# The sixth product's weight sums in five seven-product halves: all added by GpSimd, instead of two by VectorE and three by adding DMAs

## The chip, the cores and the metric

The kernel runs on one core of a Trainium2 chip. The metric is the device time of one execution in microseconds (us); lower is better. The core has a matrix engine (TensorE; PE in the profile, with PEld for its weight loads), VectorE (DVE), ScalarE (ACT), GpSimd (POOL) and SyncE (SP). DMAs that SyncE issues go through one queue, DMAs that GpSimd issues through another.

## The reference

One layer of an encoder block over 256 tokens and a width of 2048, in float32. The input `x` is normalised and multiplied by `w_in`. The eight parts of the result feed a recurrent branch (convolution, gates, two scans), an attention branch, and two merge gates. Both branches are projected, gated, added and multiplied by `w_out`.

```
xn = rms_norm(x, norm_pre_w)
u, g_lru, q, k, v, g_attn, m_lru, m_attn = split(xn @ w_in)
h   = rg_lru(conv(u), forward) + rg_lru(conv(u), backward)
y_a = h * silu(g_lru)
y_b = windowed_gqa(rope(q), rope(k), v, sink) * silu(g_attn)
merged = sigmoid(m_lru) * (y_a @ w_proj_a) + sigmoid(m_attn) * (y_b @ w_proj_b)
out = x + rms_norm(merged @ w_out, norm_post_w)
```

## The kernel before

All weights stream through once, in steps whose order is written out by hand in the strings `START`, `MERGE` and `OUT`. A step is a "block" or a "quad" of 128x2048 weights, or a "part" of the same size in a group of seven products. Each step is worked in two halves of 128x1024. For each half, ScalarE casts the raw weights to a high part `wh` (line 219), VectorE subtracts to get the low part `wl` (line 221), and PE multiplies with both. In the main loop, the cast of half `hs + 4` and the subtraction of half `hs + 3` are issued while half `hs` is multiplied, and loads are issued 3 to 5 steps ahead. Further work (convolutions, scans, attention heads, evacuations) is hung on time steps of this loop. Engines run their instructions in the order in which they are recorded.

Five halves of matrix products, named L, M, N, A (the two merge gates' columns of `w_in`) and O (half of the columns of `w_out`), are done with seven products in place of eight. Each has four blocks of weights, and some of the seven products need sums of these blocks. The sums grow in place in two cells, "x" and "y", each in two parts (0 and 1) of two tiles of 128x1024 (a and b). So `Lx0a` is tile a of part 0 of cell x of group L. SyncE loads a fresh block into a cell; the next blocks are added to it by DMAs that GpSimd issues with `accum_op=ALU.add` (line 192). Each DMA moves one tile, 512 KB.

- Cell x serves products m5, m6 and m4 in turn (in L, M, N and A its first block serves m1 too).
- Cell y is loaded fresh with the block of m3; later m7 adds to it.
- For m6, cell x needs the very block that lies fresh in cell y for m3.

In groups A and O, the table `ADDED` makes VectorE add cell y's tile to cell x's (line 224), right after it has split that tile for m3. In L, M and N the block is read from HBM a second time, by four adding DMAs per group. The split of a tile for m6 by ScalarE and VectorE waits for its sum.

The line that chooses, in `fetch`, and the add, in `split`, are in the functions printed here.

Of the kernel before, what the change touches and what calls it, by code (L numbers as in the profile page):

```python
# [18 lines left out]
ALU = mybir.AluOpType  # L19
# [50 lines left out]
LRU = (-4, 0, 2, 2, 2, 2, 2, 4)  # L70
QUADS = {"u": ("w_in", U0), "v": ("w_in", V0), "p": ("w_proj_a", 0),
         "b": ("w_proj_b", 0), "o": ("w_out", 0)}
ADDED = {'A': {'m3': 'm6'}, 'O': {'m3': 'm6'}}
PAIRS = {"g": GL0, "h": GA0, "w": U0, "k": K0, "q": Q0}
SEVENS = {"L": ("w_in", ML0 + 1024), "M": ("w_in", ML0), "N": ("w_in", MA0), "A": ("w_in", MA0 + 1536), "O": ("w_out", 0)}

# [10 lines left out]
def load_plan():  # L87

    plan = []
    for o in START + MERGE + OUT:  # L90
        a, i = o.split(".")
        if a[0] in SEVENS:
            plan.append(("part", a[0], a[1:], int(i)))
        elif a[0] in PAIRS:
            n = int(a[1:]) * (4 if a[0] == "q" else 1) + int(i)
            plan.append(("blk", "w_in", PAIRS[a[0]] + n * P, 0))
        else:
            w, c = QUADS[a[0]]
            plan.append(("quad", w, c + int(a[1:]) * 512, int(i)))
    return plan  # L100
# [15 lines left out]
def body(ctx, tc, x, x0, xT, wall, wlru, pvec, npost, ident_d, mask_d, rope_d, out):  # L116
    nc = tc.nc
# [8 lines left out]
    def unit(name, dt=F32, shape=(P, 4, S)):  # L126
        return units.tile(list(shape), dt, tag="u", name=name)
# [27 lines left out]
    plan = load_plan()  # L155
# [31 lines left out]
    def load(cell, p, add=False):  # L187

        w = wall[row[content(p)]]
        for h in range(2):  # L190
            if add:
                nc.gpsimd.dma_start(flat(cell[h]), w[:, h * 1024:(h + 1) * 1024], accum_op=ALU.add)
            else:
                nc.sync.dma_start(flat(cell[h]), w[:, h * 1024:(h + 1) * 1024])
# [3 lines left out]
    def chained(i):  # L198
        return plan[i][0] == "part" and groups[plan[i][1]].where(plan[i][2]) != "z"

    def fetch(i, lead):
        if i >= len(plan):
            return
        if plan[i][0] == "part":
            groups[plan[i][1]].fetch(plan[i], lead)
        if lead == 3 and i not in raws and not chained(i):
            nc.sync.dma_start(flat(raw_tile(i)), wall[row[content(plan[i])]])

    def split(q, c=0, w=1024, cast=nc.scalar.copy, only=None):
        i, h = q // 2, q % 2  # L210
        if i >= len(plan):
            return
        if c == 0 and only != "l":
            parts[q] = [unit(f"w{s}{i}_{h}", F32R, (P, 1024)) for s in "hl"]
        wh, wl = parts[q]
        cell = groups[plan[i][1]].cell(*plan[i][2:]) if chained(i) else raws[i]
        hs, ls, raw = wh[:, c:c + w], wl[:, c:c + w], flat(cell[h])[:, c:c + w]
        if only != "l":
            cast(hs, raw)  # L219
        if only != "h":  # L220
            nc.vector.tensor_tensor(ls, raw, hs.bitcast(F32), ALU.subtract)  # L221
            if plan[i][0] == "part" and plan[i][2] in ADDED.get(plan[i][1], ()):
                x = flat(groups[plan[i][1]].cells["x", plan[i][3]][h])
                nc.vector.tensor_tensor(x, x, raw, ALU.add)

    def mm3(ps, wh, wl, xh, xl, start, stop, more=False):

# [113 lines left out]
    def x_sum(name, s, q):  # L341
        t = unit(name, F32R, (P, 4, 2, P))
        nc.sync.dma_start(t.rearrange("p a b c -> p a (b c)").bitcast(F32), away[q][:, SUMS.index(s)])
        return t

    class Seven:
# [22 lines left out]
        def fetch(self, p, lead):  # L369
            m, q = p[2:]  # L370
            fresh = ("m1", "m3") if self.sums is None else ()
            if self.sums is None:
                if lead == 4 and m in fresh:
                    self.start(self.where(m), q)
                if lead == 4 and SEVEN[m][0][0] == "s":
                    self.kept[m, q] = x_sum(f"{self.name}{m}{q}", SEVEN[m][0], q)
            if lead == 5 and m in ("m5", "m6", "m7", "m4")[self.sums is not None:] and m not in ADDED.get(self.name, {}).values():
                load(self.cell(m, q), p, True)

        def start(self, where, q):  # L380
# [109 lines left out]
    for j in range(4):  # L490
        if j == 0:
            scale_x(0, 0, lambda: split(0, 0, 512, nc.vector.tensor_copy, "h"))
            split(0, 0, 512, only="l")
        else:
            scale_x(0, j)
            split(j // 2, j % 2 * 512, 512)
# [370 lines left out]
    def head(hd, qh, ql, b, both, end):  # L867
# [73 lines left out]
        if j % 2 == 1:  # L941
            for d, fn in enumerate((send, None, fetch, None, None, p_parts, None, None, values, gate_out), 6):
                if fn:
                    at(b + d, fn)
            if g > 1:
                at(max(b + 16, end + hd // 2 - 4), lambda: yb_parts(hd // 2))
# [196 lines left out]
    for i, (kind, half) in enumerate(steps):  # L1143
        for h in range(2):
            new = h == 0 or kind != "part"
            tick += new
            now[0], hs = tick, 2 * i + h
            if h == 0:
                for lead in (3, 4, 5):
                    fetch(i + lead, lead)  # L1150
            if new and tick in first:
                first.pop(tick)()
            if hs < FIRST:
                split(hs + 4)
            if new:
                for fn in due.pop(tick, ()):
                    fn()
            if hs >= FIRST:
                split(hs + 4, only="h")
                if hs > FIRST:  # L1160
                    split(hs + 3, only="l")
            if new and tick in last:
                last.pop(tick)()
            half(h, *parts.pop(hs))
# [72 lines left out]
```

## Time and profile before

| | |
|---|---|
| median of 3 runs | 877.22 us (876.87 to 877.27) |
| the profiled execution | 876.5 us, span 874.7 us |
| PE / VectorE / ScalarE / GpSimd busy | 864.9 / 728.6 / 643.1 / 66.1 us |
| adding DMAs on GpSimd's queue | 72, 37.75 MB |
| GpSimd's adds of two tiles | 1 (128x512, in the tail) |
| HBM read | 228.24 MB |

The span is the profiled part of an execution; the time of the whole execution lies 1.8 us above it. A row of a group names line, engine, operation, and `out<-in` by the kernel's tile names. A row of the timeline begins with start and length in us, and a number in square brackets is the idle time before it with what ended it. A row of a tile view gives shortest, median and longest duration in ns and the first and last start in us. In a row of stretches the busy times are those of PE, PEld, VectorE, ScalarE and GpSimd, each with its count of instructions, then PE's clock, the DMA share and GB/s.

### The profile page before, as it was taken

Reading aid. Unit: us, or ns where it says so; the run is one execution under the profiler, and the core shown is the slowest. Engines: PE = TensorE matmul, PEld = TensorE weight load, DVE = VectorE, ACT = ScalarE, POOL = GpSimd, SP = SyncE. Lnnn points to the kernel's source line nnn. Section 1 sums busy time; section 2 is a strip of 40 time slices with the busy share of each in tenths; the row PEclk is TensorE's granted clock in tenths of the full one; section 3 lists DMA queues with packets and bytes.
Section 4 is the critical chain, followed back from the end, with each engine's and each line's share of the span. In section 5 each row is a group of like instructions: output and inputs, shape, how many; then the busy total and the mean of one; then the engine's idle time right before and its main releaser. Section 6 shows DMA issues by size and latency. Waiting matters only on the chain.

```text
span 874.7 us, 12312 instructions
## 1 busy us (share of the span) xinstructions
PE 864.9 (99%) x4474; PEld 741.7 (85%) x4474; DVE 728.6 (83%) x975; ACT 643.1 (74%) x929; POOL 66.1 (8%) x97
## 2 busy tenths in 40 slices
PE   9999999999999999999999999999999999999996
PEld 8888888888888888888888888888888888888885
DVE  6898999898887989779677788988678778778885
ACT  7689687877888696887777699976567456555654
POOL 0000001012000011100001200000000101000200
PEclk9999999999999999999999999999999999999999
DMA  9757699999959999996999987999989988968772
GB/s 332 276 194 236 202 362 244 361 332 291 336 186 278 319 298 316 302 314 230 277 345 305 303 297 218 333 326 309 303 323 364 297 269 261 315 248 353 188 198 96
DMA packets 63390, 247.92 MB, mean 283 GB/s; under 512 B 6241, under 2 KB 19297, under 8 KB 47841
## 3 DMA queue, kind: packets, MB, share of 16 engines
q1 hardware_dynamic: 52384, 208.59, 64.6%
q0 software_dynamic: 10368, 37.75, 22.2%
q10 hardware_dynamic: 576, 0.79, 0.3%
q8 instruction: 35, 0.57, 0.2%
q14 instruction: 27, 0.21, 0.1%
HBM read 228.24 MB, written 18.87 MB: 283 GB/s over the span
## 4 chain that ended last, share of the span: by engine, by line
PE 94%; issue 3%; DMA 2%; ACT 0%; POOLq 0%; DVE 0%; SPq 0%; ACTq 0%
PE ga L255 7%; PE q L255 7%; PE gl L255 7%; PE u L255 5%; PE Am L410 4%; PE Mm L410 4%; PE Lm L410 4%; PE Nm L410 4%; PE ga L253 3%; PE q L253 3%; PE gl L253 3%; PE Om L410 3%; PE u L253 3%; PE pa__6025 L275 2%; PE pa__5514 L275 2%
## 5 line engine op out<-in xcount | busy, mean ns | idle before, releaser
L221 DVE TENSOR_TENSOR wl<-raw,wh 128x1024 fp32r<-128x1024 f32 (+1 forms) x252 | 299.1, 1203 | 56.5 <-ACT wh L219 43.9
L219 ACT CAST wh<-raw 128x1024 fp32r<-128x1024 f32 (+1 forms) x251 | 253.7, 1036 | 67.5 <-DMA raw<-wall_dram 39.6
L255 PE MATMUL ga<-xs,wh 128*128 128x512 f32 x256 | 63.5, 391 | 0.0
L255 PE MATMUL gl<-xs,wh 128*128 128x512 f32 x256 | 63.4, 391 | 0.0
L255 PE MATMUL q<-xs,wh 128*128 128x512 f32 x256 | 63.2, 391 | 0.0
L255 PEld LDWEIGHTS q<-xs,wh 128*128 128x128 f32 x256 | 47.0, 188 | 9.1
L255 PEld LDWEIGHTS gl<-xs,wh 128*128 128x128 f32 x256 | 47.0, 188 | 9.0
L255 PEld LDWEIGHTS ga<-xs,wh 128*128 128x128 f32 x256 | 46.7, 188 | 8.8
L255 PE MATMUL u<-xs,wh 128*128 128x512 f32 x192 | 47.5, 391 | 0.0
L255 PEld LDWEIGHTS u<-xs,wh 128*128 128x128 f32 x192 | 35.2, 188 | 6.7
L253 PEld LDWEIGHTS q<-xs,wl 128*128 128x128 f32 x256 | 33.2, 191 | 1.2
L253 PE MATMUL q<-xs,wl 128*128 128x256 f32 x256 | 34.0, 283 | 0.0
L253 PEld LDWEIGHTS ga<-xs,wl 128*128 128x128 f32 x256 | 33.0, 191 | 1.2
L253 PEld LDWEIGHTS gl<-xs,wl 128*128 128x128 f32 x256 | 32.8, 191 | 1.2
L253 PE MATMUL ga<-xs,wl 128*128 128x256 f32 x256 | 33.5, 283 | 0.0
L253 PE MATMUL gl<-xs,wl 128*128 128x256 f32 x256 | 33.2, 283 | 0.0
L253 PEld LDWEIGHTS u<-xs,wl 128*128 128x128 f32 x192 | 24.6, 191 | 0.9
L253 PE MATMUL u<-xs,wl 128*128 128x256 f32 x192 | 24.9, 283 | 0.0
L662 DVE SCALAR_TENSOR_TENSOR uu<-upad,pv,uu 128x256 f32<-128x256 f32 x48 | 23.2, 483 | 1.7
L746 ACT ACTIVATE sig<-sg 128x512 f32<-128x512 f32 x16 | 10.2, 635 | 14.1 <-DVE sg L589 14.1
L148 ACT CAST ms<-mt 128x512 fp32r<-128x512 f32 x8 | 4.7, 588 | 20.0 <-PE mt L989 20.0
L230 PE MATMUL gate<-ul,lwl 128*128 128x256 f32 x64 | 18.1, 283 | 0.0
(513 smaller groups left out, 2097.5 us busy)
## 6 DMA issues: line engine op xcount, KB each, us to landing
raw<-wall_dram SPq DMA_DIRECT2D x121, 1024.0 KB, 7.9
lraw<-wlru_dram SPq DMA_DIRECT2D x8, 512.0 KB, 6.3
away<-xx SPq DMA_DIRECT2D x8, 512.0 KB, 8.7
Lm<-away SPq DMA_DIRECT2D x8, 512.0 KB, 11.2
Mm<-away SPq DMA_DIRECT2D x8, 512.0 KB, 13.4
Nm<-away SPq DMA_DIRECT2D x8, 512.0 KB, 14.2
turn<-pt SPq DMA_DIRECT2D x32, 128.0 KB, 4.4
pl<-turn SPq DMA_DIRECT2D x8, 512.0 KB, 7.2
```

The costliest lines, as they stand in the source:

```text
L148: nc.scalar.copy(h, src)
L219: cast(hs, raw)
L221: nc.vector.tensor_tensor(ls, raw, hs.bitcast(F32), ALU.subtract)
L230: nc.tensor.matmul(ps, wl, xh, start=False, stop=stop, skip_group_check=more)
L253: nc.tensor.matmul(ps[:, 1], wl[:, sl], a[:, 0], start=False, stop=False)
L255: nc.tensor.matmul(ps, wh[:, sl], a, start=k == 0, stop=k == KT - 1)
L275: nc.tensor.matmul(got[t], a[:, i], (wl if low else wh)[:, sl], start=k + low + i == 0, stop=low == 1 and k == KT - 1)
L410: nc.tensor.matmul(self.ps[b], a[i], (wl if low else wh)[:, sl], start=fresh and j + low + i == 0, stop=last and j + low == 2, skip_group_ ...
L662: nc.vector.scalar_tensor_tensor(u, up[:, j, tap:tap + S], cw[:, tap:tap + 1], u, ALU.mult, ALU.add)
L746: nc.scalar.activation(sg, dst, AF.Sigmoid)
```

## The change

`ADDED` no longer names groups: for every group, the tile of m3 is added to cell x, and no adding DMA is issued for m6. The add moves from VectorE to GpSimd, at the same place in the program.

```
-ADDED = {'A': {'m3': 'm6'}, 'O': {'m3': 'm6'}}
+ADDED = {"m3": "m6"}
...
             nc.vector.tensor_tensor(ls, raw, hs.bitcast(F32), ALU.subtract)
-            if plan[i][0] == "part" and plan[i][2] in ADDED.get(plan[i][1], ()):
+            if plan[i][0] == "part" and plan[i][2] in ADDED:
                 x = flat(groups[plan[i][1]].cells["x", plan[i][3]][h])
-                nc.vector.tensor_tensor(x, x, raw, ALU.add)
+                nc.gpsimd.tensor_tensor(x, x, raw, ALU.add)
...
-            if lead == 5 and m in ("m5", "m6", "m7", "m4")[self.sums is not None:] and m not in ADDED.get(self.name, {}).values():
+            if lead == 5 and m in ("m5", "m6", "m7", "m4")[self.sums is not None:] and m not in ADDED.values():
                 load(self.cell(m, q), p, True)
```

GpSimd's queue in group L, first before, then after. `upad` is the padded buffer of the convolution, the first `Lx` rows before are the adding DMAs for m6, and the `Ly` rows those for m7.

```order
L582 MEMSET upad_1782 128x2x2
L583 MEMSET upad_1782 128x2
L192 DMA Lx0a<-wall_dram 128x1024
L192 DMA Lx0b<-wall_dram 128x1024
L192 DMA Lx1a<-wall_dram 128x1024
L192 DMA Lx1b<-wall_dram 128x1024
L192 DMA Ly0a<-wall_dram 128x1024
```

```order
L582 MEMSET upad_1782 128x2x2
L583 MEMSET upad_1782 128x2
L224 ISA
L224 TENSOR_TENSOR Lx0a<-Lx0a,Ly0a 128x1024
L224 TENSOR_TENSOR Lx0b<-Lx0b,Ly0b 128x1024
L224 TENSOR_TENSOR Lx1a<-Lx1a,Ly1a 128x1024
L224 TENSOR_TENSOR Lx1b<-Lx1b,Ly1b 128x1024
L192 DMA Ly0a<-wall_dram 128x1024
```

Four adds stand where four DMAs stood; the same exchange is made in M and N. The ISA row, which loads GpSimd's code for such adds, stood before the add in the tail and now stands before the first add of L. In A and O four adds are new in GpSimd's queue, ahead of the `Ay` and `Oy` DMAs.

VectorE's queue in group A, around the split of `Ay0a` and `Ay0b`, before:

```order
L221 TENSOR_TENSOR wl_0_6669<-Ay0a,wh_0_6668 128x1024
L224 TENSOR_TENSOR Ax0a<-Ax0a,Ay0a 128x1024
L934 TENSOR_TENSOR sga_6162<-o_6660,sga_6162 128x512
L149 TENSOR_TENSOR yb_6658<-sga_6162,yb_6658 128x2x256
L221 TENSOR_TENSOR wl_1_6679<-Ay0b,wh_1_6678 128x1024
L224 TENSOR_TENSOR Ax0b<-Ax0b,Ay0b 128x1024
```

The two rows of line 224 are gone from it after the change; the rest stands in the same order. O loses its four in the same way.

## The prediction

> **What bounds the kernel now.** I read the page first, then the waits of the matrix engine, then stretches of the span.
>
> ```profile
> PE 864.9 (99%) x4474; PEld 741.7 (85%) x4474; DVE 728.6 (83%) x975; ACT 643.1 (74%) x929; POOL 66.1 (8%) x97
> ...
> PE spin L452 <- POOL eps L454: 1.0, 1, 1.0
> PE u_ps L557 <- ACT xs L486: 0.5, 1, 0.5
> PE u_ps L557 <- ACT wh L219: 0.3, 1, 0.3
> ...
> 35.00:866.00 831.00, 831.00 (x4287) 712.40 (x4286) 699.93 (x933) 614.57 (x885) 63.71 (x84) 1.00 0.88 283
> ```
>
> The first row is the page's busy time, the next three are all of PE's waits, and the last is one stretch of 831 us (columns: length; PE, PEld, DVE, ACT, POOL busy; PE clock; DMA share). PE is busy for all 831.00 us of it at clock 1.00. Its only waits are 1.8 us at the very start. So PE's work is the time, and nothing that is made lighter on another engine or queue can shorten those 831 us. A change can lose time, by making a weight tile arrive later than PE's need of it. What has to be known is how far VectorE (DVE), which makes the low part `wl` of each weight tile, runs ahead of PE, and what the change does to that lead.
>
> **The removed transfers.** Twelve adding DMAs go: two parts of two tiles in each of L, M and N.
>
> ```profile
> q0 software_dynamic: 10368, 37.75, 22.2%
> ...
> ACT wh L219 <- DMA raw<-wall_dram: 39.6, 18, 6.5
> ```
>
> The kernel has 72 of these DMAs (37.75 MB at 512 KB each). Twelve are a sixth: 22.2% / 6 = 3.7% of the 16 DMA engines' span. Some of ScalarE's 39.6 us of waiting for raw tiles may go with them. PE waits for none of it (rows above), so I cost this at nothing; the cover is PE's own work, and if it were gone the gain could not pass ScalarE's 39.6 us.
>
> **The adds taken off VectorE.** In A and O, eight adds of one tile leave it:
>
> ```profile
> L224 DVE TENSOR_TENSOR Ax0a<-Ax0a,Ay0a x1: 1226/1226/1226, 676.6 to 676.6; 128x1024 f32<-128x1024 f32 x1
> ...
> L1108 POOLq MODIFY_POOL_CONFIG  x2: 366/366/366, 840.2 to 840.2; - x2
> L1108 POOLq EVENT_SEMAPHORE  x1: 17/17/17, 847.3 to 847.3; - x1
> L1108 POOL TENSOR_TENSOR yw<-yw,xr x1: 1265/1265/1265, 869.1 to 869.1; 128x512 f32<-128x512 f32 x1
> ...
> L454 POOL MEMSET eps<- 128x1 f32 x1 | 0.1, 99 | 0.0
> ```
>
> 8 x 1.22 = 9.8 us of VectorE, none of it on PE's path: worth nothing by itself. It comes too late to help the stretch of A below, whose first add on VectorE starts at 676.6.
>
> **The adds on GpSimd.** Twenty come, four in each of five groups. The trace has one GpSimd add of two operands, half as wide: 1.265 us. With about 0.10 us of fixed start (the smallest memset, 99 ns), a tile of 1024 columns takes 0.10 + 2 x 1.165 = 2.43 us, 49 us in all on an engine that is 8% busy. Ahead of the first one stands the loading of GpSimd's code, which before sat at 840.2 and let the next wait end at 847.3, 7.1 us later.
>
> ```profile
> L192 POOL DMA_DIRECT2D Lx1b<-wall_dram x3: 874/881/888, 149.2 to 224.3; - x3
> L194 SPq DMA_DIRECT2D Ly0a<-wall_dram x1: 327/327/327, 170.0 to 170.0; - x1
> DMA to landing us min/median/max: 9.0/9.6/10.3
> ...
> 208.38 1.07 ACT L219 CAST wh<-Lx0a 128x1024 fp32r<-128x1024 f32 x1
> ```
>
> GpSimd's last DMA of the fifth product's first use is at 149.2, and the first add needs `Ly0a`, which lands at 170.0 + 9.0 = 179.0. The code load has 30 us of cover; it costs nothing. The sums are needed from 208.4 on, when ScalarE casts `Lx0a`. Two adds after 179 and two after the next pair of tiles has landed are done before that, so they do not come late by themselves. Queued behind the four adds on GpSimd are the seventh product's adding DMAs and, in L, two memsets of the convolution's next buffer.
>
> ```profile
> L219 ACT CAST wh<-Ny0a x2: 1047/1052/1058, 468.5 to 503.2; 128x1024 fp32r<-128x1024 f32 x2
> L192 POOL DMA_DIRECT2D Ny0a<-wall_dram x1: 862/862/862, 472.7 to 472.7; - x1
> DMA to landing us min/median/max: 9.2/9.3/9.4
> ...
> 198.76 0.44 POOL L582 MEMSET upad<- 128x4 f32 x1
> ...
> 221.36 0.69 DVE L593 TENSOR_TENSOR upad<-u,upad 128x512 f32<-128x512 f32 x1
> ```
>
> N is the tightest: `Ny0a` went out at 472.7 and is cast at 503.2. Behind four adds it goes out some 8 us later, near 481, and lands 9.4 us on, 13 us ahead of the cast. The memset at 198.8 has until 221. Both cost nothing while these covers stand; gone, each would cost what it is late.
>
> **What the adds do to VectorE.** This is the term that decides. Both engines would read two operands from SBUF at the same time. The trace of before shows no such overlap, so it gives bounds only. Let h be the time for which one GpSimd add keeps VectorE from working. If they pass each other freely, h is 0. If GpSimd holds what VectorE needs for a whole add, h is 2.43. Between them lies the case where they meet only for one stream of the tile's columns, for which the nearest row is VectorE's own add of such a tile, 1.22. VectorE is nearly full where the adds fall, and the lead over PE is short. Each stretch below runs from the landing of the first fresh tile to the weight tile with the shortest lead (in A, `Ay0a` lands at 659.4 + 7.3 = 666.7):
>
> ```profile
> L194 SPq DMA_DIRECT2D Ay0a<-wall_dram x1: 332/332/332, 659.4 to 659.4; - x1
> DMA to landing us min/median/max: 7.3/9.2/11.1
> ...
> 179.00:195.00 16.00, 16.00 (x92) 14.10 (x91) 15.55 (x21) 11.44 (x15) 1.74 (x2) 1.00 1.03 346
> 318.00:341.00 23.00, 23.00 (x125) 20.00 (x124) 21.28 (x26) 19.02 (x23) 3.49 (x4) 1.00 1.05 316
> 458.00:471.00 13.00, 13.00 (x72) 11.30 (x71) 12.27 (x15) 11.05 (x17) 1.73 (x2) 1.00 1.04 295
> 666.00:675.00 9.00, 9.00 (x41) 7.38 (x40) 9.00 (x12) 6.61 (x9) 0.00 (x0) 1.00 0.93 376
> 793.00:806.00 13.00, 13.00 (x60) 10.73 (x60) 11.62 (x18) 8.83 (x14) 0.00 (x0) 1.00 0.99 401
> ```
>
> The third busy figure is VectorE's, so its idle time there is 0.45, 1.72, 0.73, 0.00 and 1.38 us. The lead is from the end of a `wl` to the first PE product that reads it:
>
> ```profile
> 193.75 1.20 DVE L221 TENSOR_TENSOR wl<-raw,wh 128x1024 fp32r<-128x1024 f32 x1
> 196.61 2.08 PE L253 MATMUL ga<-xs,wl 128*128 128x256 f32 x16
> ...
> 339.58 2.35 DVE L221 TENSOR_TENSOR wl<-raw,wh 128x1024 fp32r<-128x1024 f32 x2
> 346.37 2.08 PE L253 MATMUL ga<-xs,wl 128*128 128x256 f32 x16
> ...
> 469.92 1.22 DVE L221 TENSOR_TENSOR wl<-raw,wh 128x1024 fp32r<-128x1024 f32 x1
> 475.16 2.08 PE L253 MATMUL q<-xs,wl 128*128 128x256 f32 x16
> ...
> 674.31 1.22 DVE L221 TENSOR_TENSOR wl<-raw,wh 128x1024 fp32r<-128x1024 f32 x1
> 680.90 0.61 PE L275 MATMUL pb__6624<-wl,yb 128*128 128x512 f32 x2
> ...
> 805.82 4.65 DVE L221 TENSOR_TENSOR wl<-raw,wh 128x1024 fp32r<-128x1024 f32 x4 [1.25 <-ACT wh L219]
> 813.06 0.62 PE L410 MATMUL Om<-wl,ms 128*128 128x512 f32 x2
> ```
>
> In the first three pairs the sixteen products are the low ones of two half tiles, and this `wl` serves the second eight, which begin about 0.96 us after the row's start. Leads: L 197.57 - 194.95 = 2.6; M 347.3 - 341.9 = 5.4; N 476.1 - 471.1 = 5.0; A 680.9 - 675.5 = 5.4; O 813.1 - 807.0 = 6.0.
>
> PE's stall in a group is the time that VectorE is kept out, less its idle time, less the lead. Four adds come before the tile in question in L, M, A and O. In N the second pair lands late and I count three.
>
> - h = 2.43: L 9.72 - 0.45 - 2.6 = 6.7; M 2.6; N 7.29 - 0.73 - 5.0 = 1.6; A 4.3; O 2.3. Sum 17.5 us.
> - h = 1.22: L 4.88 - 0.45 - 2.6 = 1.8; the others come out below zero, so nothing. Sum 1.8 us.
> - h = 0: nothing.
>
> I take h = 2.0, nearer to the row of GpSimd's own add, since both of its operands stream for nearly its whole length, but less than all of it, as its start and the finish of its writes need no operand, and a few VectorE instructions in the stretches read one operand from PSUM. Then L 8.0 - 0.45 - 2.6 = 4.95, M 0.9, N 0.3, A 2.6, O 0.6: 9.35 us.
>
> [...]
>
> The profiled execution took 876.5 us by itself (span 874.7), 0.7 us under the median 877.22 of the runs shown. 876.5 + 9.35 = 885.9 us.
>
> **The rivals.**
>
> *GpSimd and VectorE pass each other.* Then no lead is used up and the time stays at 876.5 to 877.2 us, not slower. It decides in L: below h = (0.45 + 2.6) / 4 = 0.76 us no tile there comes late, and nowhere else. For it: an engine that adds at half VectorE's rate may leave VectorE most of what it needs. Against it: nothing in the trace.
>
> *VectorE goes first and GpSimd waits.* VectorE's rows follow each other without a pause, so an add would start only in a gap. Then the sums come later, against ScalarE's cast at 208.4 in L, 29 us after the first could start. VectorE idles 0.45 us in the first 16 us of these. The third and fourth add of a group could be late by an add or two, 2.4 to 5 us, of which the lead of that cast over PE hides most: 877 to 880 us. [...]
>
> *Faster.* Fewer transfers or a lighter VectorE would have to shorten PE's work. With PE busy for all of 35 to 866 us, what is left is the start, which the change does not touch, and the tail, whose rows are the same: at most a few tenths, 876 us.
>
> *The change does not do what it says* (a GpSimd add far over 2.43 us, or code loaded again for each group): 20 longer adds would bring h above 2.43 and the time over 893 us.
>
> **How the numbers follow.** Forecast (VectorE kept out, PE stalls in L and A above all): 0.62. Passing freely: 0.23. VectorE first: 0.09, half of it within 0.2%. Faster: 0.03. Dearer than 893: 0.03. A change of 0.2% (1.75 us) is about what a measurement of this kernel can tell from none. Slower by more: 0.62 + 0.05 + 0.03 = 0.70; within: 0.23 + 0.04 = 0.27; faster: 0.03. The range starts at 876.0, where the free passing lies, and ends at 893, a little under 876.5 + 17.5. The forecast's own range is 878.3 to 893.
>
> **What would show it.** Right: VectorE rows of 2 to 3.6 us beside the adds where they took 1.22, GpSimd adds of 2.4 us or more, and PE waits for `wl` near 185 to 200 and 670 to 685 us that were not there before. Wrong: `wl` rows still at 1.22 us beside the adds and PE busy throughout; or adds that start long after their tiles have landed; or PE waits that name `wh` of the sixth product, which would mean late sums.

## The result: 1.3 to 1.6% slower, lost in short waits of PE beside the adds

The changed kernel took 890.26 us (median of 4 runs, 888.47 to 890.82) against 877.05 us (4 runs, 876.86 to 877.27): a ratio of 1.0146, 95% interval 1.013 to 1.0161. Its profiled execution took 890.41 us (span 888.3, 13.6 us longer than before).

The page of after, its busy times and GpSimd's DMA queue:

```profile
PE 870.2 (98%) x4474; PEld 744.7 (84%) x4474; DVE 757.0 (85%) x967; ACT 643.4 (72%) x929; POOL 116.2 (13%) x105
...
q0 software_dynamic: 8640, 31.46, 18.4%
```

GpSimd is busy for 50.1 us more: its 20 adds take 60.9 us, and the twelve DMA issues that are gone had taken 10.7. VectorE has eight instructions less and is still busy for 28.4 us more: something lengthens its other work. GpSimd's queue lost a sixth of its transfers, as foreseen. PE's waits in after, in all, their count and the longest (before had only those of the first microseconds):

```profile
PE Lm L410 <- DVE wl L221: 2.8, 1, 2.8
PE q L253 <- DVE wl L221: 1.8, 1, 1.8
PE Am L410 <- DVE wl L221: 1.2, 1, 1.2
...
PE gate L229 <- DVE ul L149: 0.9, 1, 0.9
PE o L229 <- DVE pl L149: 0.8, 1, 0.8
...
PE ga L253 <- DVE wl L221: 0.6, 1, 0.6
PE Mm L410 <- DVE wl L221: 0.5, 1, 0.5
```

All seven name an output of VectorE, none a `wh` of the sixth product: PE never waits for a sum. They add up to 8.6 us. The timeline of group L in after shows how one arises (start, length):

```profile
177.66 7.93 DVE L221 TENSOR_TENSOR wl<-raw,wh 128x1024 fp32r<-128x1024 f32 x3
178.01 3.15 POOL L224 TENSOR_TENSOR Lx0a<-Lx0a,Ly0a 128x1024 f32<-128x1024 f32 x1 [27.39 <-DMA Ly0a<-wall_dram]
181.12 3.40 POOL L224 TENSOR_TENSOR Lx0b<-Lx0b,Ly0b 128x1024 f32<-128x1024 f32 x1
...
190.89 3.30 POOL L224 TENSOR_TENSOR Lx1a<-Lx1a,Ly1a 128x1024 f32<-128x1024 f32 x1 [6.38 <-DMA Ly1b<-wall_dram]
191.86 3.41 DVE L149 TENSOR_TENSOR lwl<-lraw,lwh 128x1024 fp32r<-128x1024 f32 x1
195.19 1.21 DVE L221 TENSOR_TENSOR wl<-Lx1b,wh 128x1024 fp32r<-128x1024 f32 x1
196.46 1.22 PE L410 MATMUL Lm<-wl,Lm 128*128 128x512 f32 x2 [2.84 <-DVE wl L221]
196.49 2.75 POOL L224 TENSOR_TENSOR Lx1b<-Lx1b,Ly1b 128x1024 f32<-128x1024 f32 x1 [2.30 <-DVE wl L221]
196.93 0.68 DVE L593 TENSOR_TENSOR sg<-gl,sg 128x512 f32<-128x512 f32 x1
197.64 2.14 DVE L589 TENSOR_TENSOR sg<-sg,rbc 128x512 f32<-128x512 f32 x1
```

Three subtractions at 1.22 us, each starting 1.13 us after the last, take some 3.5 us; here they took 7.93, so two adds cost VectorE 4.4. The `lwl` row took 3.41 in place of 1.22: 2.19 more. The `sg` row took 2.14 where its kind took 0.69. The row at 196.93, which reads one operand from PSUM (`gl`), lies inside an add and keeps its 0.68. Over all 20 adds VectorE's rows are 38.8 us longer than the same forms before, 1.94 us an add, and up to 2.22 where a two-operand row of 1024 columns was met.

How much later PE starts its products than in before, by group (differences of the first product's start of each half of a step, read from both traces):

| group | forecast, us | measured, us | PE's waits there in after |
|---|---|---|---|
| L | 4.95 | 4.41 + 0.73 | Lm 2.8, ga 0.6 |
| M | 0.9 | 2.02 | Mm 0.5, gate 0.9 |
| N | 0.3 | 1.95 + 1.65 | q 1.8 |
| A | 2.6 | 1.10 + 1.48 | o 0.8, Am 1.2 |
| O | 0.6 | 0 | none |
| sum | 9.35 | 13.3 | 8.6 |

The waits give 8.6 us of it, and at each of the seven the next product starts another 0.2 to 0.3 us later than the idle time shows. Stretches of the span show a further share (length; PE, PEld, VectorE, ScalarE, GpSimd busy; PE clock; DMA share, GB/s). After:

```profile
192.54:195.96 3.42, 1.08 (x5) 0.56 (x3) 3.42 (x2) 0.25 (x1) 1.65 (x1) 1.00 0.84 347
195.96:199.37 3.41, 2.91 (x11) 2.72 (x12) 3.38 (x4) 0.00 (x0) 2.75 (x1) 0.50 0.15 40
...
469.02:472.44 3.42, 1.63 (x13) 1.39 (x12) 3.42 (x3) 0.00 (x0) 1.56 (x1) 1.00 0.00 0
472.44:475.85 3.41, 3.41 (x14) 2.93 (x13) 3.41 (x5) 2.19 (x5) 0.00 (x0) 0.50 0.76 293
```

Behind the two longest waits PE runs for 3.41 us at clock 0.50. That is up to 1.7 us of its work each time. The prediction had no term for it. Part of it only stands in place of later waits, as the run of L, M and N alone shows below.

### The profile page after: what moved, and what is told of

Read it like the earlier page. It is cut to its first block, busy times and chain, and to the rows that moved or that the text cites. A ratio compares the mean times of both kernels' runs of the same rounds, so it can differ in the third digit from the quotient of the medians.

```text
span 888.3 us, 12289 instructions
## 1 busy us (share of the span) xinstructions
PE 870.2 (98%) x4474; PEld 744.7 (84%) x4474; DVE 757.0 (85%) x967; ACT 643.4 (72%) x929; POOL 116.2 (13%) x105
## 4 chain that ended last, share of the span: by engine, by line
PE 87%; DVE 6%; issue 3%; DMA 2%; ACT 1%; POOLq 0%; ACTq 0%; DVEq 0%; SPq 0%
PE q L255 6%; PE ga L255 6%; PE gl L255 6%; PE u L255 5%; PE Am L410 4%; PE Lm L410 4%; PE Nm L410 4%; PE Mm L410 3%; PE Om L410 3%; DVE wl L221 3%; PE q L253 3%; PE ga L253 3%; PE gl L253 3%; PE u L253 3%; PE pa__6025 L275 2%
## 5 line engine op out<-in xcount | busy, mean ns | idle before, releaser
L221 DVE TENSOR_TENSOR wl<-raw,wh 128x1024 fp32r<-128x1024 f32 (+1 forms) x252 | 314.1, 1263 | 49.6 <-ACT wh L219 36.4
L229 PE MATMUL gate<-ul,lwh 128*128 128x256 f32 x64 | 18.6, 291 | 0.9 <-DVE ul L149 0.9
```

Source lines behind the costliest of these rows:

```text
L229: nc.tensor.matmul(ps, wh, xl, start=False, stop=False, skip_group_check=more)
```

## The experiments

The main theory, from the rows above (1.94 us an add, and the row that reads `gl` from PSUM unchanged at 0.68): a GpSimd add that reads SBUF and a VectorE instruction with two SBUF operands cannot run together, each add keeps VectorE out for about 2 us, and where that exceeds the lead of a tile, PE waits. The rivals: the loss comes from fewer transfers or the new order of the queues, from any GpSimd instruction at all, from GpSimd's time alone, or from the clock.

**All five groups on VectorE** (the same source of the sums, the other engine):

```diff
-                nc.gpsimd.tensor_tensor(x, x, raw, ALU.add)
+                nc.vector.tensor_tensor(x, x, raw, ALU.add)
```

> All twenty adds on VectorE, no adding DMA for the sixth product (twelve fewer, as in the changed kernel). Shut-out theory (GpSimd's adds keep VectorE out): nobody is shut out; VectorE gets 1.13 us more per add in L, M and N, at the split of the fresh tile, where its lead over PE is 6 to 8 us; two adds are 2.3 us. No stall: 876.5 to 877.5 us. Rival (the loss comes from the sums' new source or the missing DMAs and their order in GpSimd's queue): about 890 us still.

876.43 us against 876.79 us, ratio 0.9994 (0.9985 to 1.0004): no loss. Its busy times:

```profile
PE 864.5 (99%) x4474; PEld 741.9 (85%) x4474; DVE 742.0 (85%) x987; ACT 643.6 (74%) x929; POOL 55.6 (6%) x85
```

VectorE carries 13.4 us more than before and PE loses nothing. So dropping the twelve transfers neither costs nor brings anything, and the loss comes from the engine that adds.

**The two halves of the change.** GpSimd in A and O alone, on the kernel before; and in L, M and N alone, on the kernel after:

```diff
 before.py
-                nc.vector.tensor_tensor(x, x, raw, ALU.add)
+                nc.gpsimd.tensor_tensor(x, x, raw, ALU.add)
 after.py
-                nc.gpsimd.tensor_tensor(x, x, raw, ALU.add)
+                (nc.vector if plan[i][1] in "AO" else nc.gpsimd).tensor_tensor(x, x, raw, ALU.add)
```

> The adds of A and O alone move from VectorE to GpSimd; L, M and N keep their adding DMAs. Shut-out theory: A's stalls of the changed kernel (1.1 and 1.5 us) come back and nothing else: 879 to 880 us. VectorE instructions beside the eight adds up to 2.2 us longer. Rival (transfers or L, M, N's order): 877 us.

> The adds of L, M and N on GpSimd, those of A and O on VectorE as before. Shut-out theory, with the losses adding up: L 5.3, M 2.0, N 3.6 us of the changed kernel: 887 to 888 us. If the stretches depend on each other (a late kernel has more lead later): 889 to 891 us.

The first took 878.7 us (1.0022, 1.0013 to 1.0031), the second 887.4 us (1.0122, 1.0107 to 1.0137), against 876.79 us. The excesses, 1.9 and 10.6 us, sum to 12.5 of the change's 13.2: the groups are nearly independent. The first lies a little below the 879 to 880 us expected, the second within its range. PE's waits in the first, behind the kernel's start, of which A has all:

```profile
PE Am L410 <- DVE wl L221: 1.2, 1, 1.2
...
PE o L229 <- DVE pl L149: 0.3, 1, 0.3
```

The wait at `o`, 0.8 us in after, is 0.3 here. In the second, PE came later by 5.0 us in L, 2.1 in M and 2.6 to 2.9 in N, and no stretch at clock 0.50 followed any wait in its profile. In L the sum is that of after (5.0 against 5.1) without the slow clock: there the slow stretch of after only stood in place of further waits, since the next tile was late anyway. In N it is 0.7 to 1.0 less than in after. There PE has a second wait, of 0.55 us, at the tile used at 476 in before, on which the prediction's sum for N stood; after has the slow clock in its place:

```profile
PE q L253 <- DVE wl L221: 2.3, 2, 1.8
```

**Reading one operand, and none.** The add replaced by a copy of the fresh tile, and by a memset:

```diff
-                nc.gpsimd.tensor_tensor(x, x, raw, ALU.add)
+                nc.gpsimd.tensor_copy(x, raw)
 (and, in the other kernel)
+                nc.gpsimd.memset(x, 0.0)
```

> As the changed kernel, but GpSimd copies the fresh tile over cell x's where it added them: one operand read in place of two (the sixth product's weights are then not the sum). If the reading of SBUF is what collides: a VectorE instruction with two SBUF operands waits for the copy as it waited for the add, for the copy's length, which I estimate from the 482 ns copy of 256 columns at 1 to 1.9 us; h about 1 to 1.5: 877.5 to 881 us. If only a GpSimd instruction with two operands collides: no VectorE row longer than in before, 876.5 to 877.5 us.

> As the changed kernel, but GpSimd sets cell x's tile to zero where it added: it writes a tile and reads none (the sixth product's weights are then zero). If it is GpSimd's reading that keeps VectorE out: memsets of about 0.9 us (204 ns for 128 columns, 99 for one) and no VectorE row longer than in before beside them; 876.5 to 877.5 us. If any use of SBUF by GpSimd does: a VectorE row 0.6 to 0.9 us longer beside each memset, as the copies made it 0.84 us longer; the time would stay, since the copies' did.

With copies 876.72 us against 876.79 us (0.9997, 0.9988 to 1.0007), with memsets 876.82 us against a median of 876.59 us: neither costs anything that shows. For the copies 877.5 to 881 us was expected if reading collides, so the time missed it; VectorE's rows are longer, as that theory had it, but by less than the 1 to 1.5 us it gave. The memsets' kernel ran once. The copies' tile view (shortest, median, longest in ns), then a memset and the row that VectorE starts during it:

```profile
L224 POOL COPY Lx0b<-Ly0b x1: 1985/1985/1985, 179.5 to 179.5; 128x1024 f32<-128x1024 f32 x1
...
L224 POOL COPY Mx0a<-My0a x1: 1040/1040/1040, 317.9 to 317.9; 128x1024 f32<-128x1024 f32 x1
```

```profile
671.78 0.96 POOL L224 MEMSET Ax1b<- 128x1024 f32 x1 [3.12 <-DVE wl L221]
...
672.24 1.22 DVE L221 TENSOR_TENSOR wl<-raw,wh 128x1024 fp32r<-128x1024 f32 x1
```

A copy takes 1.04 us alone and, but for the one below, up to 2.1 beside VectorE. The copies lengthen VectorE's rows by 11.2 us in all, at most 0.84 each (1.22 to 2.06). PE does not wait: in L, where the prediction's lead is shortest, the four cost VectorE 2.6 us against 0.45 us of idle time and 2.6 of lead. The memsets take 0.95 to 0.97 us. They need no fresh tile and start earlier (172.3 us in L), but 29 rows of VectorE run beside them, six two-operand rows of 1024 columns begin during one, and none is longer by more than 0.01 us. So in these runs it is reading, not writing or being busy, that shuts VectorE out: its rows are longer by up to 2.22 us beside adds, which read two operands, by up to 0.84 beside copies, which read one, and by at most 0.01 beside memsets. The PSUM row at 196.93 us, which kept its 0.68 us inside an add, agrees with the theory's second condition, two SBUF operands on VectorE's side.

One copy shows the other order, in the timeline of the copies' kernel:

```profile
678.96 6.64 POOL L224 COPY Ax1a<-Ay1a 128x1024 f32<-128x1024 f32 x1 [8.62 <-DVE sga L934]
679.47 1.22 DVE L221 TENSOR_TENSOR wl<-Ay0b,wh 128x1024 fp32r<-128x1024 f32 x1
680.61 1.22 DVE L221 TENSOR_TENSOR wl<-raw,wh 128x1024 fp32r<-128x1024 f32 x1
681.74 0.68 DVE L149 TENSOR_TENSOR yb<-sga,yb 128x512 fp32r<-128x512 f32 x1
682.35 2.35 DVE L221 TENSOR_TENSOR wl<-raw,wh 128x1024 fp32r<-128x1024 f32 x2
```

Five VectorE instructions pass at their usual 1.22 and 0.68 us while this copy takes 6.64 us, 5.6 more than one alone. The 20 adds of after took 2.39 to 3.41 us, so none waited more than about 1.0 us, less than one VectorE row of 1.22. What lets VectorE keep its turn here was not found.

**The same reading in four pieces.** Each add as four of 256 columns (lines from 224 on are one higher):

```diff
-                nc.gpsimd.tensor_tensor(x, x, raw, ALU.add)
+                for c4 in range(0, w, 256):
+                    nc.gpsimd.tensor_tensor(x[:, c4:c4 + 256], x[:, c4:c4 + 256], raw[:, c4:c4 + 256], ALU.add)
```

> The changed kernel with each add cut into four of 256 columns (about 0.68 us each alone). If GpSimd gets its turn after each VectorE instruction and then holds it out: each VectorE instruction beside the pieces 0.5 us longer, some 40 us in all as with whole adds (38.8), but spread over four times as many VectorE instructions, so that idle time and leads absorb more of it and the single stalls are shorter: 883 to 888 us. If short pieces slip in between: VectorE rows unchanged and 876.5 to 878 us.

882.96 us against 876.59 us (1.0066, 1.005 to 1.0082), at the lower edge of the range expected. Timeline of group L, and PE's waits:

```profile
177.28 5.13 DVE L221 TENSOR_TENSOR wl<-raw,wh 128x1024 fp32r<-128x1024 f32 x3
177.92 5.08 POOL L225 TENSOR_TENSOR Lx0a<-Lx0a,Ly0a 128x256 f32<-128x256 f32 x3
...
184.99 1.75 DVE L221 TENSOR_TENSOR wl<-raw,wh 128x1024 fp32r<-128x1024 f32 x1
```

```profile
PE ga L254 <- DVE wl L221: 2.1, 1, 2.1
...
PE Lm L411 <- DVE wl L221: 1.0, 1, 1.0
```

Now piece and VectorE instruction take turns, each subtraction is longer by 0.54 us, and the loss halves. VectorE's rows are 34 us longer in all, near the 38.8 of whole adds, but the delay is spread over more rows, so that idle time and leads absorb more of it. The price is per piece that VectorE meets, as the theory has it.

**The leads by themselves.** On the kernel before, VectorE's own subtraction repeated at seven places far from the groups, which delays it by known amounts without GpSimd:

```diff
+PROBE = {((START + MERGE + OUT).index(s), h): k for s, h, k in (
+    ("h4.0", 1, 3), ("g10.1", 1, 4), ("h14.1", 1, 4), ("q2.1", 1, 6), ("p0.2", 1, 8), ("p3.0", 1, 3), ("b2.0", 1, 6))}
...
-            nc.vector.tensor_tensor(ls, raw, hs.bitcast(F32), ALU.subtract)
+            for _ in range(1 + PROBE.get((i, h), 0)):
+                nc.vector.tensor_tensor(ls, raw, hs.bitcast(F32), ALU.subtract)
```

> The kernel before with no change but at seven places far apart: there VectorE makes the same low part 4 to 9 times in place of once (h4.0 +3, g10.1 +4, h14.1 +4, q2.1 +6, p0.2 +8, p3.0 +3, b2.0 +6, each in the second half), 34 instructions of 1.135 us more, none on GpSimd. By the lead rule (extra time, less idle, less lead) PE stalls there for 0.6, 1.2, 2.2, 1.8, 2.9, 1.4 and 4.0 us: 14.0 us in all. If the half-speed clock of 3.4 us after the changed kernel's two longest stalls is a consequence of them, it follows stalls of about 2 us and more here too, at 1.7 us each: three to four of them, 895 to 898 us. If it was chance: clock 1.00 throughout and 890 to 891 us. If leads don't matter (a stall begins at once): 915 us.

906.05 us against 876.59 us (1.0337, 1.0319 to 1.0356): a miss by 8 us or more. Place by place, stall expected and measured: h4.0 0.6 and 1.0, g10.1 1.2 and 1.8, h14.1 2.2 and 2.7, q2.1 1.8 and 2.6, p0.2 2.9 and 6.3, p3.0 1.4 and 0.95, b2.0 4.0 and 4.75. Of the six other sums five are 0.4 to 0.8 us too low and one 0.45 too high; the one that fails is p0.2 (this kernel's lines are up to 3 higher):

```profile
PE pa__5531 L278 <- DVE ya L151: 6.2, 1, 6.2
PE pb__7158 L278 <- DVE wl L224: 4.6, 1, 4.6
```

PE waited there not for `wl` but for a left operand, `ya`, queued behind it on VectorE, whose lead I had not worked out. And behind these two waits the clock fell to 0.50 for 6.83 us each. Behind those of 2.5 and 2.4 us (h14.1 and q2.1) it did not fall, against what was expected.

**The changed kernel twice more**, unaltered, for the clock:

> The changed kernel once more, unaltered, for a second profile: does the half-speed clock of 3.41 us that followed the stalls of 2.84 us (first matmul of tile h6) and 1.8 us (q1) in its first profile come again? If it is set by the stall alone, it stands again behind both, and the span is 888 us as before. If it depends on something besides that the program does not fix, one or both are gone, or stand behind other stalls, and the span is shorter by about 1.7 us for each that is gone (427 less 227 ns a matmul over 3.41 us), 885 us where both are. The stalls themselves, and VectorE's rows of up to 2.2 us beside the adds, come back in every profile.

> The same kernel a third time, for a third profile: the same two theories as for the second, with the same numbers.

Spans 886.7 and 889.0 us. The second profile has the two slow stretches again, behind the same waits. The third has one only: behind its wait of 1.8 us in `q` there is none, and in L it comes later. Its span is not shorter for that, as it has waits in L that the others lack:

```profile
178.20 2.54 POOL L224 TENSOR_TENSOR Lx0a<-Lx0a,Ly0a 128x1024 f32<-128x1024 f32 x1 [28.16 <-DMA Ly0a<-wall_dram]
...
185.20 1.21 PE L253 MATMUL gl<-xs,wl 128*128 128x256 f32 x8 [2.10 <-DVE wl L221]
```

VectorE stood 1.2 us further back here than in before and PE no further, so the first two adds struck the rows of both halves of this `gl` tile (3.43 and 3.40 us). In after only one add struck them, and the second half was ready 0.4 us before PE came to it. PE came later by 8.2 us in L in this profile, 1.6 of them at clock 0.50. So not even the waits are the same in every run. Stretches of the third profile:

```profile
200.95:204.36 3.41, 1.80 (x13) 1.37 (x12) 3.41 (x5) 3.41 (x5) 0.00 (x0) 1.00 0.04 14
204.36:207.78 3.42, 3.42 (x14) 2.94 (x13) 3.42 (x4) 2.54 (x6) 1.25 (x2) 0.50 0.83 273
...
470.60:474.01 3.41, 2.10 (x14) 1.70 (x12) 3.41 (x3) 0.32 (x1) 2.41 (x1) 1.00 0.00 0
474.01:477.42 3.41, 2.94 (x17) 2.61 (x18) 3.41 (x5) 1.36 (x4) 0.00 (x0) 1.00 0.52 163
```

So the clock does not follow from the wait's length alone. In the trace of after the slow clock begins at 195.96 and 472.44 us, in the probe's at 580.22 and 757.71. It fell at the end of before too, at 871.15 us, behind 3.41 us in which PE did nothing. In the 3.41 us ahead of the slow clock PE was busy for 1.08 and 1.63 us in after, 1.16 and 1.64 in the second profile, 1.80 in the third, 0.00 and 0.83 in the probe: it fell also where PE had worked for half of that time. But in the probe the clock stayed at 1.00 behind 3.41 us with 1.63 us busy (from 498.30). Behind the wait of 1.8 us in `q` it fell in the first two profiles, and stayed at 1.00 in the third and in the kernel of L, M and N alone. What decides it besides the wait, no run shows.

No kernel tried beats the one before. PE is busy throughout there and has no wait to remove; of the kernels that keep the sums, only the one that adds on VectorE equals it.

## Why the prediction was right, and where its terms were wrong

*What bounds the kernel: right.* PE's work was the time, and neither fewer transfers nor a changed load on VectorE moved it (all adds on VectorE: 0.9994).

*What costs nothing: right.* The code load stands 28 us ahead of the first add, which waited for its tile alone:

```profile
L224 POOLq MODIFY_POOL_CONFIG  x2: 385/385/385, 150.2 to 150.2; - x2
```

No wait of PE names a sum, a seventh-product tile or the convolution's buffer.

*h, taken as 2.0: right.* 1.94 on the mean of the 20 adds, 2.2 beside wide rows. That an add's start and the finish of its writes need no operand was my estimate; no run shows when within an add its operands are read. What the runs show is that no VectorE row of after lost more than 2.22 us to an add, 0.17 less than the shortest add took (2.39). Both engines' orders occur: VectorE's rows were longer beside the adds, and once a copy was longer, by 5.6 us. The adds took 2.39 to 3.41 us, and I put the difference, 1.02 us, down to a VectorE row (1.22) that had begun before.

*L, 4.95: right in size, in after.* With 2.2 for each of four adds the sum would be 8.8 - 0.45 - 2.6 = 5.75. Measured 5.1, of which 2.84 came earlier than I had put it, at `Lm`, after three adds. In after part of the 5.1 is the slow clock, but L, M and N alone lost 5.0 there without it. The 8.2 us of the third profile began at a `gl` tile whose lead the prediction had not worked out.

*M, 0.9 against 2.0: mis-sized by h and by a lead left out.* 8.8 - 1.72 - 5.4 = 1.7. The larger of the two waits is for `ul`, a left operand of the gates, not for a `wl`.

*N, 0.3 against 3.6: the step that failed.* I had taken the lead from the tile used at 476, 5.0 us. A shorter one stood 14 us earlier in before:

```profile
459.08 1.22 DVE L221 TENSOR_TENSOR wl<-raw,wh 128x1024 fp32r<-128x1024 f32 x1
...
461.31 2.08 PE L253 MATMUL q<-xs,wl 128*128 128x256 f32 x16
```

Its lead is 461.31 + 0.96 - 460.30 = 2.0 us. In after, two adds struck the rows ahead of it, of 0.42 us before:

```profile
466.25 2.08 DVE L847 TENSOR_TENSOR kr<-kr,table 128x256 f32<-128x256 f32 x1
468.02 2.56 POOL L224 TENSOR_TENSOR Nx0b<-Nx0b,Ny0b 128x1024 f32<-128x1024 f32 x1
468.26 2.61 DVE L848 TENSOR_TENSOR kr<-kr,table 128x256 f32<-128x256 f32 x1
...
472.06 1.79 PE L253 MATMUL q<-xs,wl 128*128 128x256 f32 x8 [1.79 <-DVE wl L221]
```

1.66 + 2.19 - 2.0 = 1.85, measured 1.95. The other 1.65 us is the slow clock behind it. The tile at 476 did stall PE where that clock was absent, for 0.55 us in the run of L, M and N alone, so the term that I had was real and the larger one was missing.

*A, 2.6 in all: right in size, wrong in place.* I had four adds ahead of one tile. In after they fall in two pairs, of which each uses up a lead that I had not worked out:

```profile
682.32 3.42 DVE L149 TENSOR_TENSOR pl<-pl,ph 128x1024 fp32r<-128x1024 f32 x1
...
685.80 0.51 PE L229 MATMUL o<-pl,vh 128*128 128x512 f32 x1 [0.82 <-DVE pl L149]
...
695.43 3.44 DVE L221 TENSOR_TENSOR wl<-Ay0b,wh 128x1024 fp32r<-128x1024 f32 x1
...
698.92 0.74 PE L410 MATMUL Am<-wl,Am 128*128 128x512 f32 x2 [1.19 <-DVE wl L221]
```

That the two waits come to my sum is chance. *O, 0.6 against 0:* two adds, not four, came ahead of its tile, since the second pair of tiles is split only near 820 us.

*The sum, 885.9 against 890.26:* short by 4.4 us. N makes 3.3 of it (1.6 to 1.7 by its lead, 1.65 by the clock) and M 1.1; A and L are about even, and O was 0.6 too high. The rest is in the base: the median of the runs before lies 0.6 us above the execution on which the sum stood.

## What to carry to other kernels

An add moved to an idle GpSimd was not free for VectorE here: adds of two SBUF tiles of 128x1024 floats made the VectorE rows with two SBUF operands that they met longer, by 1.94 us an add, more than the 1.2 us that VectorE would have spent on it itself. Copies, which read one tile, did so by 0.56 us each (11.2 over 20), memsets by nothing that shows. Before moving one, list the lead of everything that VectorE hands to the critical engine, left operands as well as weight tiles, over the whole stretch in which the adds can fall. A stall of PE can cost more than its own length: behind 1.6 to 3.4 us of it within 3.41 us, PE ran here for 3.41 us more at clock 0.50 (6.83 in the probe), up to 1.7 us of its work for each 3.41, in some runs and not in others.

## What was not expected of the hardware

The clock fell to 0.50 behind stalls of PE, for 3.41 us in three profiles of the changed kernel and for 6.83 us in the probe, also where PE had been busy for up to 1.80 of the 3.41 us before; of four waits of 1.8 us in `q`, two were followed by it. A GpSimd copy, once, took 6.64 us in place of 1.04 beside rows of VectorE that followed each other without a pause, though the longest of 20 adds took only 1.02 us more than the shortest.
